# A two-layer block on one core: modulation columns held back, head norms by tokens, convolutions without padded copies, gate functions grouped by kind

## The chip, the cores and the metric

The kernel runs on one core of one Trainium2 chip. The metric is the device time of one launch in microseconds (us); smaller is better. The engines are named as in the profile: PE is TensorE's matmul (PEld its weight load), DVE is VectorE, ACT is ScalarE, POOL is GpSimd, SP is SyncE, which issues most DMAs. L104 is line 104 of the kernel before.

## What is computed

Tokens T = 512, width D = 1024, float32. Two layers run one behind the other; the change touches the first part of the first.

```python
ada = silu(c) @ w_ada + b_ada
sh1, sc1, g1, sh2, sc2, g2 = split(ada, 6)
h = rmsnorm(x, norm1_g) * (1 + sc1) + sh1
gate_b, gate_c, xa, xr, gr = split(h @ w_in)
y_a = gate_b * causal_dwconv(gate_c * xa, conv_a_w)
xr = causal_dwconv(xr, conv_b_w) + conv_b_b
r, i = sigmoid(xr @ w_r + b_r), sigmoid(xr @ w_i + b_i)
a = exp(-8 * r * softplus(-lam))
u = sqrt(1 - a * a) * (i * xr)
y_b = scan(a, u) * gelu(gr)
y = concat(head_rmsnorm(y_a), head_rmsnorm(y_b)) @ w_out
x = x + g1 * y
h2 = rmsnorm(x, norm2_g) * (1 + sc2) + sh2
x = x + g2 * peer(h2)
```

`peer` finds 16 of 128 x 128 experts for each token and head by two top-16 searches over sub-keys, and sums gelu(u . h2) * v over them. The second layer (attention over blocks and a gated delta rule) follows and is not touched.

## The kernel before, in words

Activations lie with channels on the 128 partitions and the 512 tokens along the row, in eight blocks of channels. A product in nearly full precision is made of three fp32r matmuls (`_mm3`, L108): weights and activations are split into a rounded part H (a copy on ACT) and a remainder L (a subtraction on DVE; `_split`, L100), and H*H, H*L and L*H are summed in a PSUM bank. `_Weights` (L120) hands out the weight chunks in a fixed order: two raw loads on SP's queue and two split chunks ahead.

The kernel is written as a list of operations; a scheduler puts them into each engine's queue by its own timeline, and an engine then runs its queue strictly in order. Where the text says `tc.issue_after(x)`, the operations in the block come behind x in the queue of x's engine, and only there.

`_phase1` (L217) is the first layer up to h2:

- `c` is loaded, passed through silu and spread over all partitions with a ones matmul (`cb`, L236). `ada(s, dc)` (L239) loads 128 rows of the transposed modulation matrix (512 KB, three buffers), multiplies them on DVE with `cb` and sums along the row: one of 48 columns, six groups of eight (sh1, sc1, g1, sh2, sc2, g2).
- The norm: squares on ACT (L258), added up on DVE (L261), four matmuls with a ones column give the sums by token (`_token_sums`, L151), root on ACT and reciprocal on DVE (`_rstd`, L163). `_row_of` (L169) spreads the four columns of inverse norms over a [128, 512] row: identity times column on DVE, then one fp32 ones matmul. `_row_by_transposes` (L180) does the same with four TensorE transposes of a broadcast column.
- The first projection (L278): per block of x the two columns, two DVE passes (L287, L288), the split, and 24 matmuls into eight banks (`zp` four, `np` two, `gp` two), which become xr and gate_c.
- Each xr bank is copied into a padded buffer (L338; two buffers, `pad` L313) and convolved in four DVE passes (`conv`, L318). Two fp32 matmuls per block give the gates (L343), sigmoids L345, then tanh L351, exponential L352, root L358, scan L360. sqrt(1 - a*a) is made as sqrt((1 + a*a) * tanh(k r)).
- `zchunk` (L306) projects one further chunk of 128 channels (24 matmuls, a `zp` bank): four for xa (L365, multiplied with gate_c into a padded buffer and convolved), four for the gelu gate (L392), four for gate_b (L400).
- `headnorm` (L372) for each branch: a matmul with a 0/1 matrix gives the squares' sum by head, [8, 512] (L378); root (L380) and reciprocal (L381) on 8 partitions; a matmul with K = 8 per block spreads them again (L385); then product and split.
- The output projection (L411 to L421), x + g1 * y (L423), the norm row again (L429), and h2 in H and L parts (L432 to L439).

`_peer` (L523) routes and runs the expert loop (L719): 128 rounds of weights and products, and beside them 256 gathers of rows on POOL for the first 128 tokens (`gather`, L695), whose `row` buffers (four) then take x again (`x2T`, L767). `_mixer2` (L773) is the second layer; L837 reads g2.

## Time and profile before

| | us |
|---|---|
| median of 3 runs | 1889.33 (1887.18 to 1890.7) |
| the profiled execution | 1889.39 |
| its span | 1887.6 |
| PE busy | 1798.1 (95%) |
| DVE busy | 1495.1 (79%) |
| ACT busy | 838.9 (44%) |
| POOL busy | 328.1 (17%) |

All times in rows are from one profiled execution, counted from its span's start. A busy PE is not PE at its peak, since matmuls overlap: pace is read from start to start. [...] A wait stands with the engine that idled, and what ended it.

### The profile page before, as it was taken

Reading aid. Unit: us, or ns where it says so; the run is one execution under the profiler, and the core shown is the slowest. Engines: PE = TensorE matmul, PEld = TensorE weight load, DVE = VectorE, ACT = ScalarE, POOL = GpSimd, SP = SyncE. Lnnn points to the kernel's source line nnn. Section 1 sums busy time; section 2 is a strip of 40 time slices with the busy share of each in tenths; the row PEclk is TensorE's granted clock in tenths of the full one; section 3 lists DMA queues with packets and bytes.
Section 4 is the critical chain, followed back from the end, with each engine's and each line's share of the span. In section 5 each row is a group of like instructions: output and inputs, shape, how many; then the busy total and the mean of one; then the engine's idle time right before and its main releaser. Section 6 shows DMA issues by size and latency. Waiting matters only on the chain.

```text
span 1887.6 us, 26152 instructions
## 1 busy us (share of the span) xinstructions
PE 1798.1 (95%) x9545; PEld 1541.1 (82%) x9545; DVE 1495.1 (79%) x3045; ACT 838.9 (44%) x1186; POOL 328.1 (17%) x260
## 2 busy tenths in 40 slices
PE   6979999999996999999999999999999999999988
PEld 4756678999985999999999999988887788767778
DVE  8995589999998988888878888889945774565665
ACT  4473343456883433333333333333334753454453
POOL 0000000000000035444444444445400000000000
PEclk9989899999997999999999999999999999999999
DMA  8951323335668979999999999999952321111022
GB/s 305 314 195 56 140 82 102 118 134 201 255 236 277 291 245 380 338 344 338 330 343 344 341 336 338 342 331 343 345 182 77 103 76 56 56 45 45 12 78 90
DMA packets 153412, 404.28 MB, mean 214 GB/s; under 512 B 12097, under 2 KB 64577, under 8 KB 151746
## 3 DMA queue, kind: packets, MB, share of 16 engines
q1 hardware_dynamic: 114690, 243.20, 37.6%
q0 software_dynamic: 36864, 134.23, 19.6%
q10 hardware_dynamic: 1728, 25.17, 3.4%
q8 instruction: 75, 1.23, 0.3%
q14 instruction: 55, 0.45, 0.1%
HBM read 370.05 MB, written 32.51 MB: 213 GB/s over the span
## 4 chain that ended last, share of the span: by engine, by line
PE 78%; DVE 10%; ACT 3%; issue 1%; DMA 1%; DVEq 0%; ACTq 0%; SPq 0%
PE pv L738 9%; PE pv L741 9%; PE pv L744 9%; PE psS L112 8%; PE psS L110 8%; PE psS L111 8%; PE ps_p L110 3%; PE ps_p L111 3%; PE ps_p L112 3%; PE ps_inv L930 2%; DVE wL L104 2%; PE ps_g L652 2%; PE ps_zp L110 1%; PE ps_zp L112 1%; PE ps_zp L111 1%; DVE ohB L632 1%
## 5 line engine op out<-in xcount | busy, mean ns | idle before, releaser
L103 ACT ACTIVATE wH<-wraw 128x1024 fp32r<-128x1024 f32 x204 | 216.6, 1062 | 426.7 <-PE psS L111 268.2
L112 PE MATMUL psS<-hidH,wL 128*128 128x384 f32 x1024 | 347.1, 339 | 3.5 <-DVE wL L104 3.5
L110 PE MATMUL psS<-hidH,wH 128*128 128x384 f32 x1024 | 347.1, 339 | 3.5 <-ACT ring L546 3.5
L111 PE MATMUL psS<-hidL,wH 128*128 128x384 f32 x1024 | 346.4, 338 | 0.0
L104 DVE TENSOR_TENSOR wL<-wraw,wH 128x1024 fp32r<-128x1024 f32 x204 | 249.4, 1223 | 97.0 <-ACT wH L103 96.8
L699 POOL DMA_INDIRECT row<-uN,uidx x128 | 161.4, 1261 | 863.0 <-DVE vidx L692 681.7
L738 PE MATMUL pv<-vH,cH 128*128 128x512 f32 x768 | 223.6, 393 | 15.9 <-ACT vH L103 15.9
L744 PE MATMUL pv<-vH,cL 128*128 128x512 f32 x768 | 237.5, 390 | 0.0
L741 PE MATMUL pv<-vL,cH 128*128 128x512 f32 x768 | 237.4, 390 | 0.0
L103 ACT ACTIVATE cH<-ring 128x384 fp32r<-128x384 f32 x128 | 67.2, 525 | 326.3 <-PE pv L741 308.5
L110 PEld LDWEIGHTS psS<-hidH,wH 128*128 128x128 f32 x1024 | 193.7, 189 | 7.8 <-ACT ring L546 4.4
L112 PEld LDWEIGHTS psS<-hidH,wL 128*128 128x128 f32 x1024 | 193.3, 189 | 5.2 <-DVE wL L104 5.0
L708 POOL DMA_INDIRECT row<-vR,vidx x128 | 166.5, 1300 | 172.1 <-DVE acc L714 150.2
L111 PEld LDWEIGHTS psS<-hidL,wH 128*128 128x128 f32 x1024 | 193.4, 189 | 3.2
L738 PEld LDWEIGHTS pv<-vH,cH 128*128 128x128 f32 x768 | 143.7, 189 | 41.0 <-ACT vH L103 16.2
L104 DVE TENSOR_TENSOR vL<-vraw,vH 128x1024 fp32r<-128x1024 f32 x128 | 156.5, 1222 | 20.6 <-ACT vH L103 20.3
L744 PEld LDWEIGHTS pv<-vH,cL 128*128 128x128 f32 x768 | 144.1, 188 | 31.0
L741 PEld LDWEIGHTS pv<-vL,cH 128*128 128x128 f32 x768 | 144.1, 188 | 31.0
L714 DVE SCALAR_TENSOR_TENSOR acc<-row,act,acc 128x1024 f32<-128x1024 f32 x127 | 162.6, 1281 | 8.1 <-DMA row<-vR,vidx 7.4
L701 DVE SCALAR_TENSOR_TENSOR row<-row,h2tok 128x1024 f32<-128x1024 f32 x128 | 154.7, 1219 | 13.2 <-DMA row<-uN,uidx 12.9
L103 ACT ACTIVATE vH<-vraw 128x1024 fp32r<-128x1024 f32 x128 | 135.8, 1061 | 0.0
L104 DVE TENSOR_TENSOR cL<-ring,cH 128x384 fp32r<-128x384 f32 x128 | 71.0, 556 | 61.7 <-ACT cH L103 61.5
(416 smaller groups left out, 3041.4 us busy)
## 6 DMA issues: line engine op xcount, KB each, us to landing
wraw<-uT SPq DMA_DIRECT2D x128, 512.0 KB, 5.6
vraw<-vR SPq DMA_DIRECT2D x128, 512.0 KB, 6.3
wraw<-w_in SPq DMA_DIRECT2D x52, 512.0 KB, 3.7
wada<-wada SPq DMA_DIRECT2D x48, 512.0 KB, 4.8
gd<-st ACTq DMA_DIRECT2D x12, 2048.0 KB, 7.3
g<-gd SPq DMA_DIRECT2D x32, 768.0 KB, 9.3
wraw<-w_out SPq DMA_DIRECT2D x16, 512.0 KB, 3.5
wraw<-w_q SPq DMA_DIRECT2D x8, 512.0 KB, 3.5
```

Of the source, the lines that this page charges most:

```text
L103: copy = nc.scalar.activation(out=H, in_=src, func=AF.Copy)
L104: nc.vector.tensor_tensor(out=L, in0=src, in1=H.bitcast(F32), op=OP.subtract)
L110: nc.tensor.matmul(out=ps, lhsT=lH, rhs=rH, start=start, stop=False)
L111: nc.tensor.matmul(out=ps, lhsT=lH, rhs=rL, start=False, stop=False)
L112: nc.tensor.matmul(out=ps, lhsT=lL, rhs=rH, start=False, stop=stop)
L699: nc.gpsimd.indirect_dma_start(out=row, out_offset=None, in_=I["uN"], in_offset=bass.IndirectOffsetOnAxis(ap=uidx[:, n:n + 1], axis=0))
L701: nc.vector.scalar_tensor_tensor(out=row, in0=row, scalar=1.0, in1=h2tok, op0=OP.mult, op1=OP.mult, accum_out=act0[:, n:n + 1])
L708: nc.gpsimd.indirect_dma_start(out=row, out_offset=None, in_=k.vrows, in_offset=bass.IndirectOffsetOnAxis(ap=vidx[:, n:n + 1], axis=0))
L714: nc.vector.scalar_tensor_tensor(out=k.acc0, in0=row, scalar=act0[:, n:n + 1], in1=k.acc0, op0=OP.mult, op1=OP.add)
L738: nc.tensor.matmul(out=pv[b][h], lhsT=cH[:, bs], rhs=vH[:, h * 512:(h + 1) * 512], start=first, stop=False)
L741: nc.tensor.matmul(out=pv[b][h], lhsT=cH[:, bs], rhs=vL[:, h * 512:(h + 1) * 512], start=False, stop=False)
L744: nc.tensor.matmul(out=pv[b][h], lhsT=cL[:, bs], rhs=vH[:, h * 512:(h + 1) * 512], start=False, stop=last)
```

## The change

- Start: a root of `eps` is taken at once, so that ACT loads the root table early; silu(c) is also written to DRAM (`cd`) from ACT's queue. The norm row is made by `_row_by_transposes`, here and before the second norm.
- First projection: one DVE pass (x * A * row) instead of two; the shift goes into ACT's rounded copy and into DVE's remainder. `mod`, behind which the next block's pass comes, is now that remainder. For block 0 the row is read from PSUM. A1 is made in one operation from a prepared G1. The softplus of lambda comes on DVE behind the last `mod`.
- The padded copies go: `conv` takes the PSUM bank (xr) or an unpadded buffer (xa), makes the first product with ACT, and the other passes are shifted in their ranges.
- Gates: the four tanh come behind the last sigmoid on ACT, the first exponential behind the last tanh.
- `headnorm`: 16 matmuls with two columns put the sums by token on 128 partitions; root and reciprocal are [128, 32]; per block ACT spreads the values and four transposes give the row. The constant `cs` and its load go.
- Modulation: groups 2, 3 and 4 stand behind both headnorms in the text, and on DVE behind the last convolution (`conv_end`). Group 5 is made at the end of the expert loop once the gathers are through, at two columns a round, in `row` buffers, with `cb` read back from `cd`.

The diff, cut:

```diff
@@ -214,6 +212,13 @@
+def _modulation_column(k, w, cb, n):
+
+    o = k.ada[:, n:n + 1]
+    k.nc.vector.scalar_tensor_tensor(out=w, in0=w, scalar=1.0, in1=cb, op0=OP.mult, op1=OP.mult, accum_out=o)
+    return o
+
+
@@ -230,6 +235,9 @@
         nc.scalar.activation(out=c1, in_=c1, func=AF.Silu)
+        root = p1.tile([P, 1], F32, name="root")
+        nc.scalar.activation(out=root, in_=k.eps, func=AF.Sqrt)
+        nc.scalar.dma_start(out=k.cd, in_=c1)
@@ -239,13 +247,12 @@
             nc.sync.dma_start(out=w, in_=I["wada"][s * 8 + dc])
-            o = k.ada[:, s * 8 + dc:s * 8 + dc + 1]
-            nc.vector.scalar_tensor_tensor(out=w, in0=w, scalar=1.0, in1=cb, op0=OP.mult, op1=OP.mult, accum_out=o)
-            return o
-
-        def ada_group(s):
-            for dc in range(KC):
-                ada(s, dc)
+            return _modulation_column(k, w, cb, s * 8 + dc)
+
+        def ada_group(s, after):
+            with tc.issue_after(after.ins):
+                for dc in range(KC):
+                    ada(s, dc)
@@ -265,41 +272,45 @@
             sqs.clear()
-            return _row_of(k, p1, pps, r, "np", 2)
+            return _row_by_transposes(k, pps, lambda tb: r[:, tb:tb + 1].broadcast_to([P, P]), "np", 2)
...
             add_square(dc)
+
+        G1 = p1.tile([P, 8], F32, name="G1")
+        nc.vector.scalar_tensor_tensor(out=G1, in0=k.col("b_ada", 8, 8), scalar=1.0, in1=k.col("norm1_g"),
+                                       op0=OP.add, op1=OP.mult)
         row = tile_("rrow", "rrow", 1)
-        nc.scalar.activation(out=row, in_=rms_row(), func=AF.Copy)
+        rps = rms_row()
+        nc.scalar.activation(out=row, in_=rps, func=AF.Copy)
...
             sc, sh = ada(1, dc), ada(0, dc)
-            nc.vector.tensor_tensor(out=sc, in0=sc, in1=k.col("b_ada", 8 + dc, 1), op=OP.add)
...
             A = A1[:, dc:dc + 1]
-            nc.vector.scalar_tensor_tensor(out=A, in0=sc, scalar=1.0, in1=k.col("norm1_g", dc, 1),
-                                           op0=OP.add, op1=OP.mult)
+            nc.vector.scalar_tensor_tensor(out=A, in0=sc, scalar=k.col("norm1_g", dc, 1), in1=G1[:, dc:dc + 1],
+                                           op0=OP.mult, op1=OP.add)
...
             with tc.issue_after(mod.ins) if dc else ExitStack():
-                nc.vector.tensor_tensor(out=t, in0=xT[:, dc, :], in1=row, op=OP.mult)
-            mod = nc.vector.tensor_scalar(out=t, in0=t, scalar1=A, scalar2=sh, op0=OP.mult, op1=OP.add)
+                nc.vector.scalar_tensor_tensor(out=t, in0=xT[:, dc, :], scalar=A, in1=row if dc else rps,
+                                               op0=OP.mult, op1=OP.mult)
             with tc.issue_after(k.weights.last.ins) if dc else ExitStack():
-                _split(k, t, hH[:, dc, :], hL[:, dc, :])
+                nc.scalar.activation(out=hH[:, dc, :], in_=t, func=AF.Identity, bias=sh)
+                mod = nc.vector.scalar_tensor_tensor(out=hL[:, dc, :], in0=t, scalar=sh, in1=hH[:, dc, :].bitcast(F32),
+                                                     op0=OP.add, op1=OP.subtract)
...
-        kc_ = _softplus(k, p1, k.neglam, 4, "lru_k")
+        with tc.issue_after(mod.ins):
+            kc_ = _softplus(k, p1, k.neglam, 4, "lru_k")
...
         nc.vector.tensor_scalar(out=nkc, in0=kc_, scalar1=-1.0, scalar2=None, op0=OP.mult)
-        cs = p1.tile([P, 32 + 4 * P], F32, name="cs")
-        nc.sync.dma_start(out=cs, in_=I["cs"])
-        sel = cs[:, 0:32].rearrange("p (j h) -> p j h", h=8)
-        selT = cs[0:8, 32:].rearrange("p (j c) -> p j c", c=P)
+        heads2 = k.heads2
@@ -310,21 +321,17 @@
-        def pad(n):
-            t = tile_("pad", "pad", 2, (P, 3 + T))
-            nc.vector.memset(t[:, 0:n], 0.0)
-            return t
-
         def conv(o, src, n, w, j, bias):
+
...
             if bias is not None:
-                nc.vector.tensor_scalar(out=o, in0=src[:, n:n + T], scalar1=wc(n), scalar2=bias,
-                                        op0=OP.mult, op1=OP.add)
+                nc.scalar.activation(out=o, in_=src, func=AF.Identity, scale=wc(n), bias=bias)
             else:
-                nc.vector.tensor_scalar(out=o, in0=src[:, n:n + T], scalar1=wc(n), scalar2=None, op0=OP.mult)
+                nc.scalar.activation(out=o, in_=src, func=AF.Copy, scale=wc(n))
             for i in range(n - 1, -1, -1):
-                nc.vector.scalar_tensor_tensor(out=o, in0=src[:, i:i + T], scalar=wc(i), in1=o,
-                                               op0=OP.mult, op1=OP.add)
+                z = n - i
+                k.conv_end = nc.vector.scalar_tensor_tensor(out=o[:, z:T], in0=src[:, 0:T - z], scalar=wc(i),
+                                                            in1=o[:, z:T], op0=OP.mult, op1=OP.add)
@@ -334,22 +341,23 @@
         for j in range(4):
-            xp = pad(3)
-            nc.scalar.activation(out=xp[:, 3:], in_=xr[j], func=AF.Copy)
-            xc.append(conv(tile_("xc", "xc", 4), xp, 3, "conv_b", j, k.col("conv_b_b", j, 1)))
+            xc.append(conv(tile_("xc", "xc", 4), xr[j], 3, "conv_b", j, k.col("conv_b_b", j, 1)))
...
                 o = tile_("gate", "gate%d" % g, 4)
-                nc.scalar.activation(out=o, in_=ps, func=AF.Sigmoid, bias=k.col(b, j, 1))
+                gate = nc.scalar.activation(out=o, in_=ps, func=AF.Sigmoid, bias=k.col(b, j, 1))
...
+        with tc.issue_after(gate.ins):
+            for j in range(4):
+                tt.append(tile_("th", "th", 4))
+                gate = nc.scalar.activation(out=tt[j], in_=rr[j], func=AF.Tanh, scale=kc_[:, j:j + 1])
         for j in range(4):
-            tt.append(tile_("th", "th", 4))
-            nc.scalar.activation(out=tt[j], in_=rr[j], func=AF.Tanh, scale=kc_[:, j:j + 1])
-            nc.scalar.activation(out=rr[j], in_=rr[j], func=AF.Exp, scale=nkc[:, j:j + 1])
+            with tc.issue_after(gate.ins) if j == 0 else ExitStack():
+                nc.scalar.activation(out=rr[j], in_=rr[j], func=AF.Exp, scale=nkc[:, j:j + 1])
@@ -363,27 +371,30 @@
             ps = zchunk(8 + j)
-            cp = pad(2)
-            nc.vector.tensor_tensor(out=cp[:, 2:2 + T], in0=gc[j], in1=ps, op=OP.mult)
+            cp = tile_("pad", "pad", 2)
+            nc.vector.tensor_tensor(out=cp, in0=gc[j], in1=ps, op=OP.mult)
...
-            ps = bank("np", 2)
-            for j, y in enumerate(ys()):
+            ps = bank("np", 2, (P, 4, 4, 2))
+            ys = list(ys())
+            for j, y in enumerate(ys):
...
                 nc.scalar.activation(out=sq, in_=y, func=AF.Square)
-                nc.tensor.matmul(out=ps[0:8, :], lhsT=sel[:, j, :], rhs=sq, start=j == 0, stop=j == 3)
-            r = tile_("hnr", "hnr", 2)
-            nc.scalar.activation(out=r[0:8, :], in_=ps[0:8, :], func=AF.Sqrt, scale=1.0 / 64, bias=k.eps[0:8, :])
-            nc.vector.reciprocal(out=r[0:8, :], in_=r[0:8, :])
-            for j in range(4):
-                y = (hs, cv)[m0 == 0][j]
-                ps = bank("gp", 2)
-                nc.tensor.matmul(out=ps, lhsT=selT[:, j, :], rhs=r[0:8, :], start=True, stop=True)
-                nc.vector.scalar_tensor_tensor(out=y, in0=y, scalar=k.col(gname, j, 1), in1=ps,
+                for tb in range(4):
+                    nc.tensor.matmul(out=ps[:, j, tb, :], lhsT=sq[:, tb * P:(tb + 1) * P], rhs=heads2,
+                                     start=True, stop=True)
+            r = tile_("hnr", "hnr", 2, (P, 4, 4, 2))
+            _rstd(k, r, ps, 1.0 / 64)
+            for j, y in enumerate(ys):
+                rb = tile_("rb", "rb", 2, (P, 4, 2, 64))
+                nc.scalar.activation(out=rb, func=AF.Copy,
+                                     in_=r[:, j].rearrange("p b (n o) -> p b n o", o=1).broadcast_to([P, 4, 2, 64]))
+                row = _row_by_transposes(k, pps, lambda tb: rb[:, tb].rearrange("p n o -> p (n o)"), "gp", 2)
+                nc.vector.scalar_tensor_tensor(out=y, in0=y, scalar=k.col(gname, j, 1), in1=row,
@@ -401,10 +412,8 @@
         headnorm(branch_b, "gn_b", 4)
-        g1 = ada_group(2)
         headnorm(branch_a, "gn_a", 0)
-        sh2 = ada_group(3)
-        sc2 = ada_group(4)
+        g1, sh2, sc2 = (ada_group(s, k.conv_end) for s in (2, 3, 4))
@@ -437,7 +446,6 @@
                                                         op0=OP.add, op1=OP.subtract))
-        ada_group(5)
@@ -714,7 +722,10 @@
-    gn, due = 0, 0.0
+    def row_tile(name):
+        return k.px.tile([P, D], F32, name=name, tag="row", bufs=4)
+
+    gn, n5, due = 0, 0, 0.0
@@ -761,6 +772,17 @@
                 gn += 1
+        if gn == 2 * P:
+            for n in range(n5, min(8, n5 + 2)):
+                if n == 0:
+                    cb = row_tile("cb")
+                    nc.sync.dma_start(out=cb, in_=k.cd[0].partition_broadcast(P))
+                w = row_tile("wada")
+                nc.sync.dma_start(out=w, in_=I["wada"][40 + n])
+                _modulation_column(k, w, cb, 40 + n)
+                n5 = n + 1
+    o = k.ada[:, 40:48]
+    nc.vector.tensor_tensor(out=o, in0=o, in1=k.col("b_ada", 40, 8), op=OP.add)
```

## Rows read from the trace of the kernel before

**Rows 1.** Busy time by stretch of the first stage; columns as in the first line.

```profile
core 0: us, PE busy (x) PEld busy (x) DVE busy (x) ACT busy (x) POOL busy (x), PEclk, DMA share, GB/s
25.30:71.20 45.90, 45.39 (x192) 37.14 (x193) 44.83 (x89) 13.76 (x19) 0.00 (x0) 1.00 0.87 298
71.20:100.20 29.00, 25.79 (x105) 19.29 (x104) 29.00 (x49) 20.73 (x25) 0.00 (x0) 1.00 0.87 301
100.20:134.10 33.90, 26.73 (x84) 17.44 (x84) 32.72 (x56) 27.02 (x30) 0.00 (x0) 0.85 0.64 210
134.10:172.80 38.70, 38.64 (x137) 24.38 (x137) 24.07 (x31) 12.33 (x17) 0.00 (x0) 0.96 0.20 69
172.80:229.20 56.40, 56.40 (x205) 40.14 (x204) 29.84 (x34) 20.40 (x29) 0.00 (x0) 0.91 0.30 106
229.20:238.20 9.00, 3.35 (x12) 1.50 (x11) 4.82 (x9) 3.28 (x6) 0.00 (x0) 0.73 0.37 130
```

**Rows 2.** Waits of PE from 71.2 to 229.2.

```profile
engine line waited for: us in total, times, longest us
PE ps_zp L110 <- ACT gg L394: 4.3, 2, 2.4
PE ps_gp L343 <- ACT wH L103: 2.9, 1, 2.9
PE ps_gp L343 <- DVE xc L326: 1.7, 1, 1.7
PE ps_gp L343 <- ACT gate L345: 1.2, 1, 1.2
```

**Rows 3.** Groups of DVE by line and shape, 71.2 to 229.2.

```profile
L243 DVE SCALAR_TENSOR_TENSOR wada<-wada,cb 128x1024 f32<-128x1024 f32 x24 | 29.1, 1214 | 0.1
...
L326 DVE SCALAR_TENSOR_TENSOR xc<-pad,cols,xc 128x512 f32<-128x512 f32 x12 | 8.7, 744 | 0.0
...
L423 DVE SCALAR_TENSOR_TENSOR xT<-ps_zp,ada,xT 128x512 f32<-128x512 f32 x7 | 5.3, 751 | 9.5 <-PE ps_zp L112 9.5
```

**Rows 4.** The same view of ACT.

```profile
L345 ACT ACT_TABLE_LOAD x6 | 7.7, 1283 | 0.1
```

**Rows 5.** Timeline of PE: projection, head row, transposes of the second layer, sums.

```profile
43.23 1.07 PE L110 MATMUL ps_zp<-hidH,wH 128*128 128x512 f32 x4
...
48.67 1.07 PE L110 MATMUL ps_zp<-hidH,wH 128*128 128x512 f32 x4
...
165.47 1.98 PE L385 MATMUL ps_gp<-hnr,cs 8*128 8x512 f32 x4
...
1483.22 0.60 PE L184 MATMUL ps_row<-ca,r 128*128 128x128 f32 x4
...
232.22 1.05 PE L158 MATMUL ps_ts<-ca,sq 128*128 128x1 f32 x8 [2.82 <-DVE sq L261]
```

**Rows 6.** Timeline of DVE and PE at the start.

```profile
18.83 0.69 DVE L173 TENSOR_TENSOR dg<-ca,rms 128x512 f32<-128x512 f32 x1
...
19.58 2.07 PE L176 MATMUL ps_row<-dg,ca 128*128 128x512 f32 x2 [1.58 <-DVE dg L173]
...
22.31 0.69 DVE L287 TENSOR_TENSOR xn<-xT,rrow 128x512 f32<-128x512 f32 x1
22.92 1.22 DVE L243 SCALAR_TENSOR_TENSOR wada<-wada,cb 128x1024 f32<-128x1024 f32 x1
...
24.07 0.54 DVE L288 TENSOR_SCALAR xn<-xn,A,ada 128x512 f32<-128x512 f32 x1
...
25.33 2.07 PE L110 MATMUL ps_zp<-hidH,wH 128*128 128x512 f32 x4 [3.68 <-ACT hidH L103]
```

**Rows 7.** Groups of DVE by line and shape, 0 to 26.

```profile
L200 DVE SCALAR_TENSOR_TENSOR lru_k_p<-lru_k_p,lru_k_z 128x4 f32<-128x4 f32 x8 | 1.3, 160 | 0.2
```

**Rows 8.** Timeline of SP's queue behind the last gathers.

```profile
1369.71 2.71 SPq L767 DMA_DIRECT2D x2T<-x1d  x2
```

**Rows 9.** Busy time near the expert loop's end; columns as in rows 1.

```profile
1420.00:1440.00 20.00, 20.00 (x89) 16.55 (x89) 8.73 (x10) 7.17 (x11) 0.00 (x0) 1.00 0.31 107
```

14 lines of the change are left out of this document (7 added, 7 removed).

## Prediction

> **What bounds the kernel now.** I began with the busy time by stretch, cut at the events of the first stage [rows 1]. TensorE starts the first projection at 25.3 us, ends it at 71.2, ends the output projection at 229.2 and starts the next stage at 238.2. The reader is to see three things there. The first projection has its 192 matmuls in 45.9 us and is nearly solid. From 71.2 to 134.1 VectorE is busy 61.7 of 62.9 us while TensorE is not. And from 134.1 to 229.2 VectorE is busy only 53.9 of 95.1 us: the order is bad, not the amount of work. [...]
>
> Then TensorE's waits between 71.2 and 229.2 [rows 2]: the four largest are 10.1 us, on ScalarE's results (gelu outputs, banks that sigmoids free) and on a convolution of VectorE. Behind them stand 24 modulation columns on VectorE, 29.1 us in this stretch although nobody needs most of them there [rows 3], and six table loads for the sigmoids alone, 7.7 us [rows 4].
>
> What TensorE needs at least is read from its spacing [rows 5]: 24 matmuls from 43.23 to 48.67, 5.44 us. The stretch 71.2 to 229.2 holds 20 such weight chunks, 108.8 us, and 24 fp32 products (8 gates, 8 head sums, 8 head rows) at 1.98/2 = 0.99 us, 23.8 us: 132.6 of 158.0. The other 25.4 us are lost: 10.1 idle [rows 2], and low clock. [...]
>
> **The change part by part**, against the profiled execution, 1889.39 us (span 1887.6; the median of the runs is 1889.33, so nothing has to be shifted).
>
> *Start of the first projection.* The chain is sums of squares, row of inverse norms, modulated x, matmul [rows 6]. Taken off it: the small softplus instructions, which now come behind the last modulated block; eight of them take 1.3 us among the adds [rows 7], some 15 in all, of which I take 1.5 us off the last add. The diagonal matrix, 18.83 to 19.58, goes: 0.75. The ones matmul of 2.07 becomes four transposes, 0.60 at full clock [rows 5], at most double here: 0.87. Block 0 reads the row from PSUM, so the copy between 21.65 and 22.31 is off the path: 0.66. From 22.31 to 25.33 a column stands between the two passes over x (22.92 to 24.07: 1.15); the two passes become one (0.69 + 0.54 against 0.75): 0.48. Together 5.4; the bias now in ScalarE's copy and the place of the next column can take some back: -5.0 us, ends -2.5 and -6.5. The early root table removes a load that ended before the sums did: 0. The write of c to DRAM is one issue on ScalarE's queue behind the silu, 4 KB: 0, at worst 0.4 before the squares.
>
> *First projection.* 8 x 5.44 = 43.5 against 45.9, the rest is the low start. VectorE gets less (its columns there were 20, now the 12 of this stage). The new pass waits for ScalarE's copy of the block before, about 0.9 us a block, inside some 10 us that the 8 missing columns leave free. I take -0.4, ends 0 and -1.
>
> *71.2 to 229.2.* (a) Columns of groups 2 to 4 wait on VectorE for the last convolution; queued behind them are only lower ranked things, and what waits for them is the first read of g1, half-way through the output projection. SP's queue can fill three buffers of the ring and then holds the fourth load until the first column ran; weight loads issued behind it have two chunks (10.9 us) of stock. The next late thing is VectorE itself: by the durations about 40 us of convolution, gates and scan against 30 us of TensorE, but only the PSUM banks bind, and products free these early. (b) Sigmoids, tanh and exponentials by kind: five of six sigmoid loads go, 5 x 1.283 = 6.4 us of ScalarE in the very stretch of the waits, and others with them. [...] (c) Head rows: 8 x (0.99 - 0.60) = -3.1 us; head sums by tokens: four matmuls of 1.05 us [rows 5] against 0.99, +0.5. Two long reciprocals turn into short ones, beside TensorE's work: 0. Eight broadcast copies, ScalarE, at most a square's length each, beside 11 us of products that need only the other branch: 0; without that cover 3 us. (d) The convolutions read PSUM, so four banks stay held until VectorE is through, where a copy freed them; and the softplus falls just there. I take +1.5; bounds 0 and the 12 passes' whole 8.7 us [rows 3].
>
> The VectorE rows say that reading PSUM costs nothing: 751 ns with a PSUM operand, 744 without [rows 3]. [...]
>
> Sum of the stretch: -7.6 - 4.0 - 3.1 + 0.5 + 1.5 = -12.7.
>
> *229.2 to 238.2.* The same row chain: diagonal matrix 0.75 and 0.87 for the transposes: -1.6, ends -0.5 and -2.2.
>
> *Group 5 at the end of the expert loop.* The x2T loads that follow the gathers are issued by 1372.4 [rows 8], and the loop is still at full pace from 1420 to 1440, with VectorE busy 8.73 of 20 us [rows 9]. Eight columns, 9.7 us, with loads on SP between those of vraw, fit: 0; POOL's queue is empty by then, since the columns come only when all 256 gathers are issued. If they slip to the loop's last rounds they cost up to 4 us.
>
> The stages behind 238.2 wait on nothing absolute, so they move as they are. Total: -5.0 - 0.4 - 12.7 - 1.6 = -19.7: 1869.7 us.
>
> **Rivals.** *Columns still crowd.* Released together behind the convolutions, they fall between the head products and the splits and TensorE's waits remain. For it: VectorE was full until 134. Against: the 41 free us after it. Then the start, first projection, (c), (d) and the end are left: -5.0 - 0.4 - 2.6 + 1.5 - 1.6 = -8.1: 1881.3.
>
> *Everything falls into place.* All idle and low clock go, the start is at its better end: -6.5 - 1 - 10.1 - 8.1 - 2.6 - 2.2 = -30.5: 1858.9.
>
> *Grouping does not hold.* Only the first tanh and the first exponential are tied; roots and gelus may still alternate and reload. Then about half of the idle and low clock gain goes, +5.8: 1875.5.
>
> *Columns in line on VectorE: slower.* Its own work from 71.2 to 229.2 is 115.6 us, 86.5 without columns. If each column blocks the queue for p us while its load comes, this engine needs 86.5 + 24p. It binds above 145.3 (p = 2.5), and the kernel is slower than before above 165 (p = 3.3). At 298 GB/s [rows 1] a 0.52 MB load takes 1.75 us, and the bare column 1.21, so it needs loads that don't overlap: three buffers, and weight loads between them. At p = 4: 182.5, +37.2: 1906.9.
>
> **How the numbers follow.** Forecast 0.60 (its own range 1864 to 1877), crowding 0.18, all in place 0.13, grouping lost 0.05, slower 0.04. The likeliest gives 1869.7. From 1859 to 1883 leaves out the slow case, the better half of the good one and a few points of crowding. A measurement here can tell 0.2%, 3.8 us: faster means below 1885.6. Crowding ends above that in 0.04 of its 0.18, with the tail's 4 us added. So faster 0.92, same 0.04, slower 0.04.
>
> **What would show it.** First matmul of the projection near 20.3; its end near 66; the next stage's first matmul near 218; TensorE's waits in between under 4 us; the columns of groups 2 to 4 behind the last convolution and done before the output projection's first result; four transposes of about 0.6 us; the last x2T load before the loop's end. The prediction is wrong if waits on columns, or on banks that convolutions hold, take the old waits' place, or if the time after the first stage moves by itself.

## The result and the profile after

The changed kernel takes 1864.73 us (median of 4 runs, 1863.24 to 1866.96), the kernel before 1888.26 us (median of 4, 1883.38 to 1890.70): a ratio of 0.9874, 95% interval 0.9859 to 0.9888. The forecast was 1869.7, between 1859 and 1883, and faster. The profiled execution of the changed kernel took 1863.24 us, with a span of 1861.5 against 1887.6.

The two traces, event by event (us; the events are those at which the prediction cut the first stage):

| | before | after | moved | forecast |
|---|---|---|---|---|
| first matmul of the projection at | 25.33 | 22.54 | -2.8 | -5.0 |
| first projection | 45.9 | 46.6 | +0.7 | -0.4 |
| its end to the end of the output projection | 158.0 | 139.4 | -18.6 | -12.7 |
| from there to the next stage's first matmul | 9.0 | 7.1 | -1.9 | -1.6 |
| all stages behind | 1649.4 | 1645.8 | -3.6 | 0 |

So 22.5 of the 26.1 us between the spans lie in the first stage. The same busy times by stretch as in [rows 1], with the same columns, for the changed kernel:

```profile
22.50:69.20 46.70, 46.61 (x192) 38.01 (x192) 39.37 (x83) 15.01 (x20) 0.00 (x0) 1.00 0.70 242
69.20:100.00 30.80, 28.37 (x103) 20.51 (x104) 19.11 (x26) 15.47 (x23) 0.00 (x0) 0.94 0.17 58
100.00:134.00 34.00, 31.57 (x139) 25.37 (x138) 30.87 (x45) 21.94 (x28) 0.00 (x0) 0.95 0.52 174
134.00:172.00 38.00, 37.72 (x202) 31.99 (x200) 32.84 (x56) 16.65 (x24) 0.00 (x0) 1.00 0.76 269
172.00:208.60 36.60, 34.51 (x152) 27.70 (x152) 21.66 (x28) 17.26 (x27) 0.00 (x0) 1.00 0.44 149
208.60:215.70 7.10, 2.21 (x13) 1.72 (x13) 4.10 (x7) 3.11 (x6) 0.00 (x0) 0.80 0.46 158
```

Three sums over these rows and over [rows 1] split the 19.7 us between the first matmul of the projection and the next stage (212.9 to 193.2). Length minus PE's busy time is idle time: 16.6 us before, 12.2 after, -4.4. Length times (1 - granted clock, the column PEclk) is taken as what the low clock cost, an estimate: 14.1 and 5.0, -9.1. The clock records of both traces hold two values, 1.00 and 0.50, and the column is their mean over the stretch; the 128x512 matmuls are 0.43 us apart where the changed kernel reads 0.50 (72.9 to 76.3 us) and 0.23 where it reads 1.00. What is left is work at 1.00: 182.2 and 176.0, -6.2. The split is rough in two ways. The clock's share is taken over idle time too, where it costs nothing (most of all in the last row); and neither trace has a clock record for the first matmuls of the projection, which were 0.43 us apart, as at 0.50 (last section). The reader is to see where the clock rose: the two stretches with the head norms, 0.96 and 0.91 before, now read 1.00. In the second of them TensorE had no idle time before either (56.40 of 56.40 us busy in [rows 1]). In the first the low clock before stood from 134.3 to 137.7 us, right behind a wait of 1.9 us; whether the wait brought it is not shown.

TensorE's waits between 69.2 and 208.6, the view of [rows 2] (us in total, times, longest):

```profile
PE ps_gp L348 <- ACT wH L101: 2.5, 1, 2.5
PE ps_row L182 <- ACT rb L394: 1.6, 1, 1.6
PE ps_zp L108 <- ACT wH L101: 1.5, 1, 1.5
PE ps_zp L110 <- DVE wL L102: 0.9, 1, 0.9
PE ps_zp L109 <- DVE yL L102: 0.7, 1, 0.7
```

These are 7.2 us against 10.1, at other places: a gate product at 69 us, weight splits at 115 and 117 that roots and gelus delayed, and head rows and splits at 173 and 176. The fp32 products by group, changed kernel from 69.2 to 215.6 first (gates, head sums, head rows), then the kernel before from 71.2 to 238.2 (gates, head rows, head sums):

```profile
L348 PE MATMUL ps_gp<-xc,wri 128*128 128x512 f32 x16 | 8.2, 596 | 2.5 <-ACT wH L101 2.5
L388 PE MATMUL ps_np<-ca,sq 128*128 128x2 f32 x64 | 7.5, 242 | 0.0
L182 PE MATMUL ps_row<-ca,rb 128*128 128x128 f32 x32 | 4.4, 274 | 1.6 <-ACT rb L394 1.6
```

```profile
L343 PE MATMUL ps_gp<-xc,wri 128*128 128x512 f32 x16 | 10.7, 782 | 5.8 <-ACT wH L103 2.9 <-DVE xc L326 1.7 <-ACT gate L345 1.2
L385 PE MATMUL ps_gp<-hnr,cs 8*128 8x512 f32 x16 | 9.4, 688 | 0.0
L378 PE MATMUL ps_np<-sq,cs 128*8 128x512 f32 x16 | 8.0, 594 | 0.0
```

And the start, VectorE of the changed kernel:

```profile
18.70 1.23 DVE L102 TENSOR_TENSOR wL<-wraw,wH 128x1024 fp32r<-128x1024 f32 x1 [0.63 <-ACT wH L101]
19.84 1.22 DVE L218 SCALAR_TENSOR_TENSOR wada<-wada,cb 128x1024 f32<-128x1024 f32 x1
...
20.98 0.74 DVE L298 SCALAR_TENSOR_TENSOR xn<-xT,A,ps_row 128x512 f32<-128x512 f32 x1
```

The four transposes that make the row of inverse norms start at 18.12 us and take 1.11, so the row is in PSUM at 19.2, but the pass over block 0 starts at 20.98: a weight split and the next block's column, 2.3 us, stand ahead of it.

### The profile page after: what moved, and what is told of

It is laid out like the page before. It is cut to its first block, busy times and chain, and to the rows that moved or that the text cites. A ratio compares the mean times of both kernels' runs of the same rounds, so it can differ in the third digit from the quotient of the medians.

```text
span 1861.5 us, 26283 instructions
## 1 busy us (share of the span) xinstructions
PE 1777.6 (95%) x9613; PEld 1542.2 (83%) x9613; DVE 1480.4 (80%) x3012; ACT 831.2 (45%) x1188; POOL 333.7 (18%) x260
## 4 chain that ended last, share of the span: by engine, by line
PE 84%; DVE 11%; ACT 3%; issue 1%; DMA 1%; DVEq 0%; ACTq 0%; SPq 0%
PE pv L749 10%; PE pv L752 9%; PE pv L755 9%; PE psS L110 8%; PE psS L109 8%; PE psS L108 8%; PE ps_p L109 3%; PE ps_p L108 3%; PE ps_p L110 3%; PE ps_zp L110 2%; PE ps_zp L109 2%; PE ps_zp L108 2%; PE ps_inv L952 2%; DVE wL L102 2%; PE ps_g L660 2%; DVE ohB L640 1%
## 5 line engine op out<-in xcount | busy, mean ns | idle before, releaser
L707 POOL DMA_INDIRECT row<-uN,uidx x128 | 166.4, 1300 | 831.2 <-DVE cL L102 659.0
L722 DVE SCALAR_TENSOR_TENSOR acc<-row,act,acc 128x1024 f32<-128x1024 f32 x127 | 162.6, 1280 | 11.5 <-DMA row<-vR,vidx 10.7
L752 PEld LDWEIGHTS pv<-vL,cH 128*128 128x128 f32 x768 | 144.1, 188 | 31.1
L755 PEld LDWEIGHTS pv<-vH,cL 128*128 128x128 f32 x768 | 144.1, 188 | 31.0
L663 ACT ACTIVATE st<-ps_g 128x512 f32<-128x512 f32 x96 | 96.2, 1145 | 32.3 <-PE ps_g L660 31.7
```

The costliest lines, as they stand in the source:

```text
L707: nc.gpsimd.indirect_dma_start(out=row, out_offset=None, in_=I["uN"], in_offset=bass.IndirectOffsetOnAxis(ap=uidx[:, n:n + 1], axis=0))
L722: nc.vector.scalar_tensor_tensor(out=k.acc0, in0=row, scalar=act0[:, n:n + 1], in1=k.acc0, op0=OP.mult, op1=OP.add)
L752: nc.tensor.matmul(out=pv[b][h], lhsT=cH[:, bs], rhs=vL[:, h * 512:(h + 1) * 512], start=False, stop=False)
L755: nc.tensor.matmul(out=pv[b][h], lhsT=cL[:, bs], rhs=vH[:, h * 512:(h + 1) * 512], start=False, stop=last)
```

## The experiments

All were timed in five rounds beside the kernel before, whose median was 1888.33, 1886.85 and 1888.08 us in the three groups of runs. Besides the time, each is read by the start of the next stage in its trace (215.7 changed, 238.2 before), since that leaves out what the later stages do. This start comes from one traced execution of each kernel, and what it differs by between executions of one kernel was not measured: a difference of a us or two is not secured.

| run | next stage at | time, median (range) | ratio to before, interval |
|---|---|---|---|
| u_columns | 218.7 | 1869.89 (1867.78 to 1870.74) | 0.9900 (0.9880 to 0.9921) |
| u_grouping | 218.9 | 1876.53 (1872.03 to 1878.97) | 0.9935 (0.9917 to 0.9953) |
| u_columns_grouping | 217.4 | 1867.53 (1864.17 to 1879.83) | 0.9904 (0.9879 to 0.9929) |
| b_columns | 233.2 | 1885.98 (1884.03 to 1891.23, and once 3593.32, not explained) | 0.9998 (0.9984 to 1.0011) |
| u_headnorm | 227.0 | 1876.21 (1873.34 to 1881.57) | 0.9937 (0.9917 to 0.9956) |
| b_headnorm | 228.2 | 1877.82 (1876.59 to 1878.79) | 0.9946 (0.9929 to 0.9963) |
| d_rows8 | 224.6 | 1879.72 (1875.91 to 1883.35) | 0.9955 (0.9941 to 0.9970) |
| u_conv | 208.7 | 1865.12 (1860.21 to 1868.85) | 0.9885 (0.9864 to 0.9906) |
| i_z8 | 214.7 | 1868.74 (1865.74 to 1872.03) | 0.9900 (0.9881 to 0.9918) |
| u_start | 221.8 | 1870.40 (1868.49 to 1872.96) | 0.9907 (0.9891 to 0.9923) |
| u_group5 | 221.6 | 1873.85 (1871.10 to 1876.45) | 0.9926 (0.9911 to 0.9940) |
| best | 209.7 | 1864.40 (1862.80 to 1868.14) | 0.9882 (0.9862 to 0.9903) |

**u_columns: the columns are not held.**

```
-        headnorm(branch_a, "gn_a", 0)
-        g1, sh2, sc2 = (ada_group(s, k.conv_end) for s in (2, 3, 4))
+        g1 = ada_group(2)
+        headnorm(branch_a, "gn_a", 0)
+        sh2 = ada_group(3)
+        sc2 = ada_group(4)
```

> The changed kernel with its modulation groups 2 to 4 no longer held behind the last convolution (they stand in the source where the kernel before had them). Reference: next stage's first matmul at 215.7 us in the changed kernel, 238.2 before; medians 1864.7 and 1888.3. Theory A (holding the columns is the larger part of the gain: VectorE is full from 69 to about 130 again and TensorE waits for what stands behind the columns): first matmul of the next stage at 224 to 230, time 1873 to 1879, VectorE busy over 95% from 70 to 120. Theory B (the table loads were what TensorE waited for, the columns only filled VectorE): at 216 to 219, time within 3 us of 1865. Theory C (the sum on record, where idle and low clock go by both parts in equal measure): about +5.8, 221.5, time 1870.5.

Measured: next stage at 218.7, 3.0 later; 5.2 us slower by the medians, with intervals that touch. That is theory B by the stage and C by the time; A falls. Yet VectorE is busy 45.95 of 50 us from 70 to 120 (35.17 in the changed kernel), and TensorE has one long wait where the changed kernel has a short one:

```profile
79.38 3.75 PE L347 MATMUL ps_gp<-xc,wri 128*128 128x512 f32 x4 [10.97 <-issue]
```

Columns stand between the convolutions' passes on VectorE, and the first gate product waits 11 us where it waits 2.5 in the changed kernel. The profile names no releaser; the first pass that ends a convolution is over at 79.3 us, just ahead of it. All but 3 us are won back further on. The columns here end at 105.8 us, in the changed kernel at 168.7, so they no longer stand among the head norms; that this is what wins the time back is argued, not shown. Where the columns stand moves the wait more than it removes it.

**u_grouping: the two ties are taken away.**

```
-        with tc.issue_after(gate.ins):
-            for j in range(4):
-                tt.append(tile_("th", "th", 4))
-                gate = nc.scalar.activation(out=tt[j], in_=rr[j], func=AF.Tanh, scale=kc_[:, j:j + 1])
         for j in range(4):
-            with tc.issue_after(gate.ins) if j == 0 else ExitStack():
-                nc.scalar.activation(out=rr[j], in_=rr[j], func=AF.Exp, scale=nkc[:, j:j + 1])
+            tt.append(tile_("th", "th", 4))
+            nc.scalar.activation(out=tt[j], in_=rr[j], func=AF.Tanh, scale=kc_[:, j:j + 1])
+            nc.scalar.activation(out=rr[j], in_=rr[j], func=AF.Exp, scale=nkc[:, j:j + 1])
```

> The changed kernel without the two ties that group tanh behind the last sigmoid and the exponentials behind the last tanh; columns still held. Per round of the gate loop ScalarE then has about 5.1 us of work and up to four table loads of 1.28 us, 10.2 us against TensorE's 7.4 us (a chunk of 5.44 and two gates of 0.99). Theory A (columns carry the gain, ScalarE has slack): +0 to +3 us, next stage at 216 to 219. Theory B (table loads carry it): ScalarE sets the pace of four rounds, +8 to +12 us, next stage at 224 to 228, time 1873 to 1877. Theory C (half and half): +5.8, 221.5, 1870.5.

Measured: 3.2 us later by the stage, and 11.8 slower by the medians: theory A by the one, B by the other. Of the 13.5 us between the spans, 10.3 lie behind the first stage, in stages with the same code (see the last section). The table loads did come back, on ScalarE from 65 to 125 us:

```profile
L350 ACT ACT_TABLE_LOAD x8 | 10.3, 1283 | 0.1
L357 ACT ACT_TABLE_LOAD x4 | 5.1, 1283 | 0.1
L363 ACT ACT_TABLE_LOAD x4 | 5.1, 1283 | 0.1
L402 ACT ACT_TABLE_LOAD x1 | 1.3, 1283 | 0.0
```

17 loads, 21.8 us, where the changed kernel has 6. The first stage is 3.2 longer with them. The rest of the time is not shown to be theirs.

**u_columns_grouping: both undone.**

> The changed kernel with both undone, columns not held and functions not tied. If the two parts gain independently, the loss is the sum of the two single ones; if either is enough to keep TensorE waiting, it is about the larger one; if the columns by themselves delay the softplus and with it the tanh, ScalarE's sigmoids stay together without a tie, and this kernel is not slower than the one with only the columns undone.

Measured: next stage at 217.4, 1.7 us behind the changed kernel and ahead of either single undoing; time 2.8 above it, within the intervals. The third reading holds. ScalarE's loads in the same stretch, without any tie:

```profile
L362 ACT ACT_TABLE_LOAD x2 | 2.6, 1283 | 0.0
L401 ACT ACT_TABLE_LOAD x2 | 2.6, 1283 | 0.0
L349 ACT ACT_TABLE_LOAD x1 | 1.3, 1283 | 0.0
L356 ACT ACT_TABLE_LOAD x1 | 1.3, 1283 | 0.0
```

The softplus is what ties them. With columns in the queue its chain on VectorE ends at 107 to 109 us, where the changed kernel ends it at 66, so the first tanh (107.6) comes behind the last sigmoid (103.2) without a tie:

```profile
L309 DVE TENSOR_SCALAR lru_k_p<-lru_k_p x1: 154/154/154, 107.4 to 107.4; 128x4 f32<-128x4 f32 x1
```

```profile
L310 DVE TENSOR_SCALAR lru_k_p<-lru_k_p x1: 170/170/170, 66.0 to 66.0; 128x4 f32<-128x4 f32 x1
```

(The softplus's factor of 8 in this kernel, then in the changed one: ns, and first and last start in us.) So the tie mends what holding the columns opens, and the two parts together are worth 1.7 us of the stage, once the other parts are there; the times cannot tell them from nothing.

**b_columns: the kernel before, with the columns held and nothing else changed.**

```
-        g1 = ada_group(2)
         headnorm(branch_a, "gn_a", 0)
-        sh2 = ada_group(3)
-        sc2 = ada_group(4)
+        with tc.issue_after(k.conv_end.ins):
+            g1, sh2, sc2 = (ada_group(s) for s in (2, 3, 4))
```

> The kernel before with one part of the change alone: groups 2 to 4 held behind the last convolution. Theory A (the columns carry the gain): 8 to 14 us faster than before, next stage at 224 to 230. Theory B (ScalarE's table loads bind once VectorE is free): the sigmoids still alternate with roots and exponentials, so no more than 4 us faster. Theory C: 5.8 faster, next stage at 232.4.

Measured: next stage at 233.2, 5.0 us earlier; time the same (0.9984 to 1.0011). Theory A falls. By the stage this is near theory C (232.4), by the time it is theory B. Six loads for the sigmoids are still there, and TensorE now waits 3.67 us for a gate.

**u_headnorm: head norms as before.** The function headnorm and its constants are those of the kernel before.

```
-            _rstd(k, r, ps, 1.0 / 64)
+            nc.scalar.activation(out=r[0:8, :], in_=ps[0:8, :], func=AF.Sqrt, scale=1.0 / 64, bias=k.eps[0:8, :])
+            nc.vector.reciprocal(out=r[0:8, :], in_=r[0:8, :])
...
-                row = _row_by_transposes(k, pps, lambda tb: rb[:, tb].rearrange("p n o -> p (n o)"), "gp", 2)
+                nc.tensor.matmul(out=ps, lhsT=selT[:, j, :], rhs=r[0:8, :], start=True, stop=True)
```

> The changed kernel with the head norms of the kernel before: sums by head in 8 rows, a reciprocal over 8 partitions by 512, rows by fp32 products with a constant. The sum on record gave the change -3.1 + 0.5 = -2.6 us with the reciprocals and the broadcast copies at nothing: undone +2.6, next stage at 218.3, time 1867.3. Rival (the norms by tokens also took low clock and a long reciprocal off the path): +5 to +8 us, with granted clock below 0.95 from 150 to 185. Rival (the copies on ScalarE cost what the rows give): 0.

Measured: next stage at 227.0, 11.3 later; time 11.5 longer. The rival holds, and beyond its range. The granted clock of this kernel, from 134 us on:

```profile
134.00:154.00 20.00, 20.00 (x73) 1.00 0.83 278
...
150.00:160.00 10.00, 10.00 (x31) 0.83 0.91 320
160.00:170.00 10.00, 10.00 (x27) 0.83 0.72 247
170.00:180.00 10.00, 9.88 (x38) 1.00 0.00 0
180.00:190.00 10.00, 10.00 (x24) 0.66 0.35 107
```

(PE's busy time, granted clock, DMA share, GB/s.) From 150 to 190 us 10 x (0.17 + 0.17 + 0.34) = 6.8 us are lost to the low clock, by the same estimate. In the changed kernel none are: its rows above read 1.00 from 134.0 to 208.6. By the profile's count TensorE was busy throughout when the clock fell: 10.00 of 10.00 us in each of the three windows below 1.00. What TensorE did just before, in this kernel:

```profile
150.76 1.98 PE L400 MATMUL ps_gp<-hnr,cs 8*128 8x512 f32 x4
...
152.67 1.02 PE L393 MATMUL ps_np<-sq,cs 128*8 128x512 f32 x2
...
154.24 0.63 PE L113 MATMUL ps_zp<-hidL,wH 128*128 128x512 f32 x1
...
161.40 1.12 PE L400 MATMUL ps_gp<-hnr,cs 8*128 8x512 f32 x2
...
163.12 1.12 PE L400 MATMUL ps_gp<-hnr,cs 8*128 8x512 f32 x2
...
177.79 3.22 PE L400 MATMUL ps_gp<-hnr,cs 8*128 8x512 f32 x6
```

Six fp32 passes of 8 rows or 8 columns stand in a run from 150.76 (an fp32 product is two passes: the 8 head rows are 16 matmuls in the trace); from 154.24 on matmuls are 0.43 us apart, where 0.23 is the pace while the clock reads 1.00. The other two falls, at 164 and at 181 us, come in the same way behind 8-row passes. The 8-column sums alone (L393) stand at 128.8 (four passes), 140.0 and 144.1 (two each) too, and the clock reads 1.00 there.

**b_headnorm: the kernel before, with the new head norms and nothing else changed.** The edit of u_headnorm the other way round.

> The kernel before with one part of the change alone: the head norms by tokens, short reciprocals, rows by transposes. Before: next stage at 238.2, median 1888. By the sum on record -2.6: 235.6, time 1885.4. By its undoing in the changed kernel (11.3 us of the stage, 11.5 of the time): 227, time 1877. Between the two if the columns of the kernel before stand in VectorE's queue ahead of the rows.

Measured: next stage at 228.2, 10.0 earlier; 10.3 us faster. The granted clock from 160 us on, which is 0.91 and 0.83 in the kernel before:

```profile
160.00:180.00 20.00, 20.00 (x107) 1.00 0.17 57
180.00:200.00 20.00, 18.78 (x89) 1.00 0.33 108
```

Done alone the part gives what its undoing takes: it is the largest of the change, and it does not need the others.

**d_rows8: eight products nobody reads.**

```
+                extra = pps.tile([P, T], F32, name="ps_extra", tag="gp", bufs=2)
+                nc.tensor.matmul(out=extra, lhsT=k.ones[0:8, :], rhs=rb[0:8].rearrange("p b n o -> p (b n o)"),
+                                 start=True, stop=True)
                 row = _row_by_transposes(k, pps, lambda tb: rb[:, tb].rearrange("p n o -> p (n o)"), "gp", 2)
```

> The changed kernel with eight more fp32 products of 8 rows by 512 columns, one ahead of each row of the head norms, whose results nobody reads (the transposes and the short reciprocals stay). [...] Theory 2 (the low clock came with waits behind the 3.3 us reciprocal over 8 partitions): 7.9 us and no more, next stage at 223 to 224, granted clock 0.98 or more from 140 to 170 as in the changed kernel.

Measured: next stage at 224.6, 8.9 later, time 15.0 longer (the stages behind were longer too in this execution), and the granted clock does not fall (same view):

```profile
150.00:160.00 10.00, 10.00 (x46) 1.00 0.87 305
160.00:170.00 10.00, 10.00 (x57) 1.00 0.50 188
...
180.00:190.00 10.00, 10.00 (x44) 1.00 0.25 84
```

The run also puts to the test that an 8-row product by itself brings the low clock, and this falls: with one among the transposes of 128 rows ahead of each row the clock reads 1.00 in every window of ten us from 130 to 190. Theory 2's size is nearly met (8.9 for 7.9, eight products of 0.99), but its cause is not, since TensorE did not wait in u_headnorm either. What is left are 8-row products close behind each other, alone or together with the 8-column sums, which this run does not have (two and four passes of these sums at a time left the clock at 1.00 in u_headnorm). That the old head norms bring the low clock is shown both ways; which of their products does is open.

**u_conv: padded copies back, all convolution passes on VectorE.**

```
-                nc.scalar.activation(out=o, in_=src, func=AF.Identity, scale=wc(n), bias=bias)
+                nc.vector.tensor_scalar(out=o, in0=src[:, n:n + T], scalar1=wc(n), scalar2=bias,
+                                        op0=OP.mult, op1=OP.add)
...
-            xc.append(conv(tile_("xc", "xc", 4), xr[j], 3, "conv_b", j, k.col("conv_b_b", j, 1)))
+            xp = pad(3)
+            nc.scalar.activation(out=xp[:, 3:], in_=xr[j], func=AF.Copy)
+            xc.append(conv(tile_("xc", "xc", 4), xp, 3, "conv_b", j, k.col("conv_b_b", j, 1)))
```

> The changed kernel with the padded copies back: the first convolution reads copies in SBUF that ScalarE makes, and VectorE makes the first pass of all eight convolutions again. The sum on record gave the change +1.5 us here (banks held by the convolutions), so undoing it would give -1.5: next stage at 214.2, time 1863. In the trace the first gate product and the next chunk start 2.5 us after the first projection, while the banks are held. Rival 1 (VectorE's eight passes now back cost more than the banks): they lie where VectorE is idle between 75 and 105, so 0 to +2 us. Rival 2 (banks are what TensorE waits for at 69): the 2.5 us and the low clock behind them go, -4 us.

Measured: next stage at 208.7, 7.0 us earlier than in the changed kernel; rival 2 holds, and more than its 4 us: no wait at 69, and none of the low clock behind it, and in place of the waits at 115 and 117 (2.4 us) stand two of 1.7 and 0.5. The time is the same (1865.12): the profiled execution, 1860.21, is the fastest of four, and the other three took 1865 to 1869. Where those lost it was not seen. Of the 7.0 us the wait (2.5) and the low clock behind it (0.83 from 70 to 80 us in the changed kernel, 1.00 here: 1.7) are some 4.2. The other 2.8 come later and are not taken apart. With the convolutions done earlier the held columns also start earlier, at 99.3 us in place of 112.3, and 13 of them in place of 18 start between the first head sum and the last head row. That is an effect of the edit beside the banks, and it was not tried by itself.

**i_z8: the first chunk ahead of the gate products.**

```
+        z8 = zchunk(8)
         for j in range(4):
             for g, lst, b in ((0, rr, "b_r"), (1, ii, "b_i")):
...
-            ps = zchunk(8 + j)
+            ps = zchunk(8 + j) if j else z8
```

> The changed kernel with the first chunk behind the projection issued ahead of the gate products. TensorE waits 2.5 us at 69 us, with a gate product at the head of its queue. Theory 1 (the convolutions hold the banks: the passes over the four banks alternate on VectorE, so the first bank is only free when the first convolution ends, about 71.5): nothing is gained, next stage at 215 to 217. Theory 2 (it is only the order of TensorE's queue): the 2.5 us and some 1.9 us of low clock behind them go, next stage at 211 to 212.

Measured: next stage at 214.7, and the wait stands, now by the chunk and with the convolution named:

```profile
71.32 0.47 PE L108 MATMUL ps_zp<-hidH,wH 128*128 128x512 f32 x1 [2.53 <-DVE xc L333]
```

Theory 1: it is the banks, not the order of TensorE's queue. On VectorE ten passes run from 66.48 to 73.05:

```profile
66.48 6.67 DVE L333 SCALAR_TENSOR_TENSOR xc<-ps_zp,cols,xc 128x511 f32<-128x511 f32 x10 [0.46 <-ACT xc L328]
```

The three passes of a bank are 511, 510 and 509 tokens long. In the trace the ten come as 511, 511, 510, 511, 510, 511, 509, 510, 509, 510: they take turns over the four banks, and the first that ends a bank is the seventh, from 70.43 to 71.17.

**u_start: the start of the kernel before,** with the diagonal matrix in both places, two passes per block, softplus not held.

```
-            return _row_by_transposes(k, pps, lambda tb: r[:, tb:tb + 1].broadcast_to([P, P]), "np", 2)
+            return _row_of(k, p1, pps, r, "np", 2)
...
-                nc.vector.scalar_tensor_tensor(out=t, in0=xT[:, dc, :], scalar=A, in1=row if dc else rps,
-                                               op0=OP.mult, op1=OP.mult)
+                nc.vector.tensor_tensor(out=t, in0=xT[:, dc, :], in1=row, op=OP.mult)
+            mod = nc.vector.tensor_scalar(out=t, in0=t, scalar1=A, scalar2=sh, op0=OP.mult, op1=OP.add)
...
-        with tc.issue_after(mod.ins):
-            kc_ = _softplus(k, p1, k.neglam, 4, "lru_k")
+        kc_ = _softplus(k, p1, k.neglam, 4, "lru_k")
```

> The changed kernel with the start of the kernel before: row of inverse norms by a diagonal matrix and an fp32 product, in both places; two passes over each block; softplus not held. Reference: first matmul of the projection at 22.5 us changed, 25.3 before; next stage at 215.7 and 238.2. By the sum on record (-5.0 at the start, -0.4 in the projection, -1.6 at the end): +7.0, next stage at 222.7, time 1871.7. By the first matmuls of the two traces (2.8 at the start, 1.9 at the end, the projection 0.7 longer in the changed kernel): +4.0, next stage at 219.7, time 1868.7. Rival (a later start is made up behind it, since TensorE waits at 69 us in the changed kernel anyway): +2.

Measured: next stage at 221.8, 6.1 later, time 5.7 longer: nearer the sum on record (7.0) than the difference of the traces (4.0). The first matmul is at 26.25, later than in the kernel before.

**u_group5: group 5 back behind the first stage.** The rounds of two columns leave the expert loop; at the end of the first stage's function stands instead:

```
+        for dc in range(KC):
+            ada(5, dc)
+        o = k.ada[:, 40:48]
+        nc.vector.tensor_tensor(out=o, in0=o, in1=k.col("b_ada", 40, 8), op=OP.add)
```

> The changed kernel with modulation group 5 back behind the first stage's norms, not in the expert loop. Theory (the sum on record gave its move no gain and no cost): within 1 us of the changed kernel, its columns in VectorE's idle time between 169 and 183 us. Rival 1 (it crowds the splits of the head norms: each column blocks VectorE's queue while its load comes, 1.75 us): up to 8 of them between the rows, TensorE waits 3 to 8 us more at 170 to 180. Rival 2 (in the loop the columns cost something, so the loop gets shorter without them): the time from the next stage's first matmul to the last product of the expert loop, 1211.2 us in the changed kernel and 1210.4 before, falls by 0.8.

Measured: next stage at 221.6, 5.9 later; time 9.1 longer. Rival 1 holds. TensorE's two waits that are 1.6 and 0.7 us in the changed kernel:

```profile
175.30 1.29 PE L182 MATMUL ps_row<-ca,rb 128*128 128x128 f32 x8 [3.14 <-DVE gcv L397]
...
180.55 0.79 PE L109 MATMUL ps_zp<-yL,wH 128*128 128x512 f32 x1 [3.03 <-DVE yL L102]
```

On VectorE six of the eight columns, from 169.04 to 181.67, stand between rows and splits of the head norms. The stretch from the next stage to the loop's last product (here and below, the last start of its H*H matmuls) was 1208.1 us, against 1211.2 in the changed kernel; b_columns, which has no columns in its loop either, gave 1208.5, the kernel before 1210.4 and u_grouping, with the columns, 1212.8: 3 us at most, and not told from what kernels differ by anyway.

**best: four waits at once.** The changed kernel with u_conv's edit, the first gelu held behind the last root, the second block's columns behind the first block's pass, and group 4 behind the second head norm's reciprocal.

```
+                with tc.issue_after(root_end.ins) if j == 0 else ExitStack():
+                    nc.scalar.activation(out=g, in_=ps, func=AF.Gelu_apprx_tanh)
...
+            with tc.issue_after(xn0.ins) if dc == 1 else ExitStack():
+                sc, sh = ada(1, dc), ada(0, dc)
...
+        g1, sh2, sc2 = (ada_group(s, k.hnr_end if s == 4 else k.conv_end) for s in (2, 3, 4))
```

> The changed kernel with padded copies back, the first gelu held behind the last root (two table loads less between them), the second block's columns held behind the first block's modulated x, and group 4 held behind the second head norm's reciprocal. Reference for the stage: 208.7 us with the padded copies alone. If each wait named in the traces goes: 1.0 at the start, 1.7 to 2.5 at 104 to 121, 0.8 and its low clock (1.7) at 152: next stage at 203 to 205. Time: the stages behind moved by up to 4 us between kernels with nothing of theirs changed, so 1857 to 1864, against 1865 for both the changed kernel and the one with padded copies back. Rival: the held gelu makes the second branch late and TensorE waits there instead: next stage at 208 to 211.

Measured: next stage at 209.7, time 1864.40; the rival. The start gained 1.1 us (first matmul at 21.45) and one load of each kind is left, but a gelu that comes later now holds up TensorE:

```profile
121.41 0.50 PE L108 MATMUL ps_zp<-hidH,wH 128*128 128x512 f32 x1 [1.37 <-ACT gg L414]
```

No version that was tried beats the changed kernel by more than a measurement can tell.

## Why the prediction was right, and where it was not

The sign, the range and the mechanism "less idle time and less low clock on TensorE in the first stage" were right, and the total was 5 us off. The terms of the sum were not right: errors of both signs cancelled, so that the total came so near was luck. The table sets the terms against what each undoing moved the next stage, which is a part's worth where the others are there:

| part | sum on record | shown |
|---|---|---|
| (a), (b) columns held, functions grouped | -11.6 | -1.7 |
| (c) head rows and sums | -2.6 | -11.3 |
| (d) convolutions read PSUM | +1.5 | +7.0 |
| start, projection, row at the end | -7.0 | -6.1 |
| group 5 moved | 0 | -5.9 |

The right column makes -18.0 of the 22.5 us; the rest comes of parts acting together.

*(a) and (b)* stand in the sum with -7.6 for idle time and -4.0 for low clock. No run shows these two, nor the 8.1 us of low clock in the sum of "Everything falls into place". What the traces show, by the estimate above and in the stretch of these terms (71.2 to 229.2 before, 69.2 to 208.6 after): low clock did go, from 11.7 to 3.5 us. But 6.8 us of it came back with the old head norms in u_headnorm, and the new ones alone (b_headnorm) bring the granted clock to 1.00. Idle time fell from 10.4 to 7.2 us, by 3.2 and not by 7.6: new waits came in. The sigmoids' loads went as forecast, from six to one, but that gained little: with 17 loads in place of 6 (u_grouping) the stage was 3.2 us longer. In the kernel before, with the other parts missing, holding the columns did move the stage by 5.0 us (b_columns), with no gain in the time.

*(c)* had the right mechanism and the wrong size. Rows fell from 9.4 to 4.4 us busy and sums from 8.0 to 7.5, where -3.1 and +0.5 were taken; above all, the clock behind the old products was not in the term. [Rows 1] had a sign of it: 0.91 over 56.40 us with 56.40 us busy does not look like idle time. The two reciprocals were put at nothing because they lie beside TensorE's work; that was not tested by itself.

*(d)* was inside its bounds, 0 to 8.7, but a value near the small end was taken. The four banks come free one after another only if the passes run bank by bank, and they ran in turns (i_z8). That reading PSUM costs nothing by itself was right: passes of one length took 740 ns over ps_zp and 747 over a tile in SBUF, in the changed kernel:

```profile
L333 DVE SCALAR_TENSOR_TENSOR gcv<-pad,cols,gcv 128x510 f32<-128x510 f32 x4 | 3.0, 747 | 0.1
...
L333 DVE SCALAR_TENSOR_TENSOR xc<-ps_zp,cols,xc 128x510 f32<-128x510 f32 x4 | 3.0, 740 | 0.0
```

Yet the first stage was 7.0 us shorter with the copies to SBUF back (u_conv); by the time nothing is seen of it (1865.12 against 1864.73). The part of the price that the trace shows is the wait for the held banks and the low clock behind it, 4.2 us.

*Start:* -2.8 of -5.0 at the first matmul, near the end given (-2.5). The clause "the place of the next column can take some back" was a part of the miss: it took 1.1, as best shows; the other 1.1 is not taken apart. The projection behind it did not get shorter: 14 matmuls were 0.43 us apart where 8 were before, and 0.23 is the pace behind them, so about 6 x 0.20 = 1.2 us, which the forecast (-0.4) did not have. *Group 5:* the loop took it as forecast, with its columns between 1350.7 and 1369.3 and the last x2T load issued at 1369.8, ahead of the loop's end at 1426.9. The step that failed was to credit nothing to the place it left. *Behind 238.2* the traces differ by 3.6 us, where 0 was forecast; the last section says why that is not put down to the change.

*What would show it.* Met: the columns of groups 2 to 4 ran from 112.3, where the last convolution's pass ends, to 168.7, ahead of the output projection's first read at 183.65; transposes at 0.5 us a row; x2T. Not met: first matmul at 20.3 (22.5), projection's end at 66 (69.2), waits under 4 us (7.2). "Next stage near 218" was met by a sum of wrong terms (215.7).

*Rivals.* "Columns still crowd" put (a) and (b) at 1881.3 without them; undone they gave 1867.5. "Everything falls into place" missed by 5.8 us: 7.2 us of waits stayed. "Grouping does not hold" is partly there: two roots and two gelus still alternate, and the waits at 115 and 117 come behind them. "Columns in line on VectorE" was not decisive, but its mechanism is in the trace: the second head norm's reciprocal, whose input is there at 164.1, stands behind three columns from 165.0 to 168.7, and the head rows' wait at 173.3 follows. The loads are hardly part of it: VectorE waits 0.18 us for the first of the three.

## What to carry to other kernels

When an engine is busy all through a stretch and its granted clock is still below 1.00, look at the kind of work in it and not only for a wait: here 6.8 us of low clock went with the old head norms' products. Price such work together with the clock behind it. Price parts of a change with the others already there: here, with the other parts in place, holding one kind of work back or tying another gained nothing alone, and the tie only mended what the holding opened. An operation that reads PSUM in place of a copy is to be priced by how long it holds the bank, and by the order in which its engine goes over the banks: here the instruction cost the same (740 against 747 ns), and the wait was at the banks (2.5 us).

## What the runs showed that was not expected

Stages whose code is the same differed in time from kernel to kernel. From the expert loop's last product to the end the changed kernel took 434.6 us, u_conv 438.5, u_grouping 443.3. The granted clock differs, not the waiting. The first line of each pair below runs from that product to the first solve of the next layer, where TensorE's waits are the same (0.72, 0.41, 0.21, 0.60 and 0.78 us); the second is the rest. The changed kernel first, then u_grouping:

```profile
1426.90:1515.30 88.40, 85.54 (x445) 0.98 0.21 72
1515.30:1861.50 346.20, 324.91 (x1956) 0.99 0.17 58
```

```profile
1431.70:1520.60 88.90, 86.03 (x431) 0.94 0.22 72
1520.60:1875.00 354.40, 333.36 (x1969) 0.97 0.17 57
```

Of the 8.7 us between the two kernels 8.2 lie in the second line. Its idle time is 21.3 and 21.0 us, while the low clock is 346.20 x 0.01 = 3.5 and 354.40 x 0.03 = 10.6, as near as two digits tell. Why the clock differs in stages with the same code is not known. It is a reason why a first stage that is 7 us shorter (u_conv) need not show in the time, and why the 3.6 us behind the first stage are not counted as the change's: its profiled execution was the fastest of four, and of the fourteen kernels traced here none had a shorter rest.

The second is at the start: the first 14 matmuls of the projection are 0.43 us apart, up to 28.25 us, while the window from 22.5 to 26.0 reads a granted clock of 1.00. The trace's first clock record stands at 28.56 us, just where the pace changes to 0.23; before it the row reads 1.00 for want of a record. There the pace tells the level, not the clock's row. No record is shown to be wrong here, but one is missing, and the pace is the check.

```profile
26.11 0.63 PE L109 MATMUL ps_zp<-hidL,wH 128*128 128x512 f32 x1
26.54 0.63 PE L110 MATMUL ps_zp<-hidH,wL 128*128 128x512 f32 x1
```
